# Matmuls of a hybrid mixer layer read their moving operand alternately from two halves

## The chip, the cores and the metric

The kernel is one program on one core of a Trainium2 chip. A core has TensorE (PE, with its weight loads listed as PEld), VectorE (DVE), ScalarE (ACT), GpSimd (POOL) and SyncE (SP), 16 DMA engines, the on-chip memory SBUF and the accumulation memory PSUM, which PE writes and DVE and ACT read. The metric is the device time of one execution in microseconds, as the median of several runs on the same chip.

## The reference

One layer over 512 positions of 1024 channels, in float32. Cut to what matters:

```python
h = rms_norm(x, norm_mix)
u_pool, u_lru, q, k, v, g_logits = split(h @ w_in)          # 8192 columns
gates = sigmoid(g_logits + b_gate)                           # three branches of 1024
y_pool = pool_mixer(u_pool, w_pool, pool_scale)              # causal means of 2, 4, 8, 16, minus the token
y_lru  = rglru_mixer(u_lru, conv_w, ...)                     # causal conv of width 4, two gates, linear scan
y_sb   = stick_breaking_attention(rms(q), rms(k), v)         # 8 heads of 128, strictly causal
merged = sum(gates[b] * (y[b] @ w_branch[b]) for b in range(3))
x = x + merged @ w_out
h2 = rms_norm(x, norm_ffn)
x = x + (silu(h2 @ w_ffn_gate) * (h2 @ w_ffn_up)) @ w_ffn_down   # 2816 hidden channels
```

## The kernel before

Everything is kept with channels on the 128 partitions and the 512 positions along the row, except q, k and v, which are made with positions on the partitions. Every operand is split into a high part (rounded to `float32r`) and the rest; a product is three matmuls, high x high, high x low and low x high (`mm3`, L277 to L280). ACT makes the high part of a weight tile (L111, L1403) and DVE the rest (L112, L1404). A full chunk (`chan_chunk`, L365) is 2 output tiles x 8 blocks of the inner dimension x 3 matmuls, 48 in all, each with a weight load of 128x128 and a moving operand of 128x512.

The stages follow each other on PE without a break. The times are those of the profile:

- From 5.7 us: the first two gate chunks at L701, then two more by chunks, on the unnormalised input; `gate_store` (L563) scales the result by the norm and takes the sigmoid.
- From 50.2: four chunks of the linear recurrence (`lru_chunk`, L596), with four gate chunks in between. The causal convolution reads the chunk's PSUM tile: L602 once, then L609 three times for each of two rows, shifted by 1, 2 and 3 positions. The small gates are half-height matmuls at L626, two side by side, read by ACT at L630 and L631.
- From 144.9: q, k and v in seven block products each in place of eight (`tok_product`, L788, matmuls at L798, read by `snap` L808 on ACT and `final` L813 on DVE).
- From 260.2: the third branch's gates in seven block products (`product`, L282, matmuls of 256 columns at L287).
- From 298.8: pooling chunks (`pool_chunk`, evacuated at L942, mapped by `pool_back`, L959) and two branches' projections (`branch`, merged by DVE at L379 and L383), with attention spread among them: transposes (L1018), scores (L1040, read by two sigmoids at L1050 and L1051), a reversed scan (L1054), transposes of the weights (L1067), the output (L1079, copied at L1082).
- From 488.2: the third branch's projection in seven block products, 256 columns at L1238.
- From 528.7: the output projection (read at L1291), and from 570.5 the first two chunks each of the hidden gate and hidden up projections (`fg`, `fu`, read at L1473 and L1475), during which the normalised hidden operand is made on DVE (L1336) and split.
- From 614.7: nine chunk pairs of the hidden projections in seven block products, 256 columns at L287. From 786.5 the first part of the down projection, 512 columns by `mm3`, read at L1580; from 797.6 the rest in seven block products, 256 columns at L1611.

The order is that of the program. Side work is put in queues (`bg`, `abg`) and taken from them a step at a time between groups of matmuls (`tick`, L329). Weight tiles are made ahead by `emit_next` (L261): load on SP's queue, split on ACT and DVE, three buffers deep. Readers that free a PSUM tile soon have a raised priority. Offsets within the tiles (L35 to L39) fix where operands lie.

Of the kernel before, what the change touches and what calls it, by code (L numbers as in the profile page):

```python
# [16 lines left out]
P = 128  # L17
# [50 lines left out]
def layer_kernel(ctx: ExitStack, tc: tile.TileContext, x, xt, vecs, w_in, w_qkv7, w_gate7, w_pool, w_rg, w_ig,  # L68
# [24 lines left out]
    def cols(ap, k0, nk, c0, nc_):  # L93
        return ap[k0 * P:(k0 + nk) * P, c0:c0 + nc_].rearrange("(k p) c -> p k c", p=P)

# [181 lines left out]
    def mm3(ps, lh, ll, rh, rl, start, stop, skip=False):  # L277
# [94 lines left out]
    def merge(br, c, pss, gts):  # L372
        for j in range(2):
            if br == BRANCHES[0]:
# [4 lines left out]
                dve.tensor_tensor(m, pss[j], gts[j], ALU.mult)  # L379
                merged.append(m)  # L380
            else:
                m = merged[2 * c + j]
                dve.tensor_tensor(gts[j], pss[j], gts[j], ALU.mult)  # L383
# [24 lines left out]
    with ExitStack() as first:  # L408
# [154 lines left out]
        def gate_store(br, c, pss, scaled):  # L563
            gt = b4([2, S], f"gt{br}{c}")
            for j in range(2):
                g = pss[j]
                if not scaled:
                    dve.tensor_tensor(gt[:, j, :], g, rb, ALU.mult)
                    g = gt[:, j, :]
                act(gt[:, j, :], g, AF.Sigmoid, bias=vcol("b_gate", 8 * br + 2 * c + j))  # L570
# [7 lines left out]
        def load_lru_weights():  # L578
# [3 lines left out]
            for n, src in enumerate((w_rg, w_ig)):  # L582
                bd = src.rearrange("(t two) i j -> two i t j", two=2)
                for two in range(2):
                    q, o = LH[two], LH[(n + two) % 2]
                    nc.sync.dma_start(raw[q, :, o], bd[two])
# [6 lines left out]
            for two in range(2):  # L593
                nc.sync.dma_start(bigx[LH[1 - two], :], big[LH[two], :])

        def lru_chunk(c):  # L596
# [3 lines left out]
            with tc.high_priority(EARLY):  # L600
                for j in range(2):
                    dve.tensor_scalar(xc[:, j, :], pair[:, j, :], vcol("conv_w", 24 + 2 * c + j),  # L602
# [17 lines left out]
            def gates(j):  # L620
                ct = 2 * c + j
                ps = pb.tile([P, 2, S], F32, tag="mm", name=f"lg{c}{j}")
                for n, (w, x_) in enumerate((("h", "h"), ("h", "l"), ("l", "h"))):
                    for two in range(2):
                        q = LH[two]
                        nc.tensor.matmul(ps[:, two, :], lw[w][q, ct, :], st[x_][q, j, :],  # L626
                                         start=n == 0, stop=n == 2)
                for two in range(2):
                    q, o = LH[two], LH[1 - two]
                    act(st["r"][q, j, :], ps[q, two, :], AF.Sigmoid, bias=vcol("b_rg", ct)[q, :])  # L630
                    act(st["i"][q, j, :], ps[o, two, :], AF.Sigmoid, bias=bigx[o, ct:ct + 1])  # L631
# [64 lines left out]
        for k in range(KT):  # L696
            if k % 2 == 0:
                wh, wl = weights("first", k // 2)
            for w, x_ in ((wh, 0), (wl, 0), (wh, 1)):
                for n in range(4):  # L700
                    nc.tensor.matmul(pss[n // 2][n % 2], w[:, k % 2, n * P:(n + 1) * P], hu[k][x_],  # L701
# [86 lines left out]
        def tok_product(t, nm, ps, first):  # L788
            bh, bl = BQ[WITH[nm]]
            for i in range(2):  # L790
                ah, al = weights("seven", t, nm, i)
                tick()
                for a in range(2):
                    ts_ = slice(a * P, (a + 1) * P)
                    for kk in range(2):
                        k = 2 * i + kk
                        for n, (b_, a_) in enumerate(((bh, ah), (bh, al), (bl, ah))):
                            nc.tensor.matmul(ps[:, a, :], b_[:, k, ts_], a_[:, kk, :],  # L798
# [4 lines left out]
        for t in VKQ:  # L803
# [4 lines left out]
            def snap(key, src):  # L808
                r[key] = b4([2, 512], f"r{t}{key[0]}{key[1]}")
                with tc.high_priority(EARLY):  # L810
                    act(r[key], src, AF.Copy, scale=-1.0 if key[0] else 1.0)

            def final(key, src):  # L813
                dve.tensor_tensor(r[key], r[key], src, ALU.subtract if key[0] else ALU.add)
# [89 lines left out]
    with ExitStack() as mix:  # L904
# [35 lines left out]
        def evac_u(ps, name):  # L940
            u = slot(name)
            act(u, ps, AF.Copy)  # L942
# [16 lines left out]
        def pool_back(g, j):  # L959
# [9 lines left out]
            act(yh, ps, AF.Copy, scale=sc)  # L969
            dve.scalar_tensor_tensor(yl, ps, sc, yh.bitcast(F32), ALU.mult, ALU.subtract)  # L970
# [32 lines left out]
        def head_tasks(h):  # L1003
# [28 lines left out]
            def scores(a):  # L1032
# [3 lines left out]
                for i in ZORDER[a]:  # L1036
# [3 lines left out]
                    mm3(z[:, c0:c0 + w], qh[:, ii], ql[:, ii], kh[:, 0:w], kl[:, 0:w], True, True)  # L1040
# [6 lines left out]
                for i in ZORDER[a]:  # L1047
                    _, c0, n = ZSEG[i]
                    cs = slice(c0, c0 + n)
                    act(K[:, cs], z[:, cs], AF.Sigmoid, scale=qrs[:, 1, i, h:h + 1])  # L1050
                    act(A[:, cs], z[:, cs], AF.Sigmoid, scale=qrs[:, 0, i, h:h + 1])  # L1051
# [21 lines left out]
            def yout():  # L1073
                ps = paux.tile([P, S], F32, tag="aux", name=f"py{h}")
                vh, vl = st["v"]
                for n, k in enumerate((0, 1, 2, 3)):
# [3 lines left out]
                        n == 0, n == 3)  # L1080
                ysb[h] = slot(f"ysb{h}")
                act(ysb[h], ps, AF.Copy)  # L1082
# [609 lines left out]
```

## Time and profile before

| what | value |
|---|---|
| runs | 897.85, 899.41, 897.85 us; median 897.85 |
| span of the profiled execution | 896.5 us (first to last instruction); 1.35 us below the median of the runs, which holds what lies around the span |
| PE, weight loads, DVE, ACT busy | 99%, 89%, 82%, 59% of the span |
| granted TensorE clock | full in every slice |
| matmuls | 5563, of which 2186 have 512 columns of `float32r` |
| DMA | 154.08 MB, mean 172 GB/s |

The profile gives one execution. A busy share counts the union of an engine's instructions; matmuls overlap their successors, so the distance from one start to the next tells more of PE than the duration (a matmul of 512 columns lasts 0.39 us by the page, though the next one starts long before). "Chain" is the work that ended last, followed back, and its pieces do not overlap. In a row of groups stand the line, engine, operation, the tiles written and read, shapes and count, then the busy time in us, the mean of one in ns, and the engine's idle time before them with what ended it.

### The profile page before, as it was taken

The page shows a single profiled execution, that of the slowest core. Times are in us where ns is not written, and L with a number is a line of the kernel's source. Part 1 is how long each engine was busy: PE and PEld are TensorE (multiplying, and loading weights), DVE is VectorE, ACT ScalarE, POOL GpSimd, SP SyncE. Part 2 cuts the span into 40 slices and gives each one's busy share as a digit, 9 for nine tenths or more (in the row PEclk, how much of TensorE's full clock was granted, in tenths as well). Part 3 has the DMA queues.
Part 4 walks back from the last instruction along what each step waited for, and adds up shares of the span by engine and source line. Part 5 has one row for each costly group of instructions (what it writes and reads, how often), then busy time and mean ns, then how long its engine had stood idle before and what let it go on. Part 6 is the DMA issues. An engine that isn't in the chain of part 4 may idle for free.

```text
span 896.5 us, 14227 instructions
## 1 busy us (share of the span) xinstructions
PE 891.2 (99%) x5563; PEld 795.2 (89%) x5563; DVE 739.4 (82%) x934; ACT 528.5 (59%) x730; POOL 88.8 (10%) x130
## 2 busy tenths in 40 slices
PE   9999999999999999999999999999999999999998
PEld 6888778788889888888888988889999999999998
DVE  6897897997786599967887695699988888899974
ACT  6554989546856556554664544545555555746642
POOL 1110002222323101000001100000000000021200
PEclk9999999999999999999999999999999999999999
DMA  9495336798692785734636865336443343897913
GB/s 337 141 297 167 118 114 215 217 302 252 174 276 72 217 252 175 236 108 152 205 90 154 179 190 170 106 107 169 126 131 104 95 118 97 228 243 195 186 42 118
DMA packets 116644, 154.08 MB, mean 172 GB/s; under 512 B 8161, under 2 KB 90081, under 8 KB 116577
## 3 DMA queue, kind: packets, MB, share of 16 engines
q1 hardware_dynamic: 103904, 107.30, 37.8%
q0 software_dynamic: 12528, 45.62, 21.6%
q8 instruction: 43, 0.70, 0.3%
q10 hardware_dynamic: 144, 0.26, 0.1%
q14 instruction: 25, 0.20, 0.1%
HBM read 132.71 MB, written 18.87 MB: 169 GB/s over the span
## 4 chain that ended last, share of the span: by engine, by line
PE 95%; DVE 2%; ACT 2%; issue 1%; DMA 0%; SPq 0%; DVEq 0%; ACTq 0%
PE ps_y L287 11%; PE ps_x L287 8%; PE ps_q L798 7%; PE ps_dy L1611 6%; PE ps_dx L1611 5%; PE ps_br L278 3%; PE ps_br L279 3%; PE ps_br L280 3%; PE ps_bY L1238 2%; PE ps_gate L701 2%; PE ps_gy L287 2%; PE ps_gate L280 2%; PE ps_bX L1238 2%; PE ps_gx L287 2%; PE ps_gate L278 2%; PE ps_gate L279 2%
## 5 line engine op out<-in xcount | busy, mean ns | idle before, releaser
L111 ACT ACTIVATE whi<-raw 128x1024 fp32r<-128x1024 f32 x69 | 73.1, 1060 | 85.2 <-PE ps_out L279 17.9
L112 DVE TENSOR_TENSOR wlo<-raw,whi 128x1024 fp32r<-128x1024 f32 x69 | 84.4, 1223 | 30.7 <-ACT whi L111 30.7
L112 DVE TENSOR_TENSOR wlo<-qw,whi 128x1024 fp32r<-128x1024 f32 x48 | 58.6, 1224 | 22.0 <-ACT whi L111 21.8
L111 ACT ACTIVATE whi<-qw 128x1024 fp32r<-128x1024 f32 x48 | 50.7, 1059 | 33.2 <-PE ps_q L798 15.3
L1403 ACT ACTIVATE wh_S<-w_S 128x1024 fp32r<-128x1024 f32 x36 | 38.3, 1067 | 34.4 <-PE ps_y L287 22.3
L1404 DVE TENSOR_TENSOR wl_S<-w_S,wh_S 128x1024 fp32r<-128x1024 f32 x36 | 43.8, 1222 | 5.2 <-ACT wh_S L1403 5.1
L1515 POOL DMA_DIRECT2D dw<-in_w_down_dram x20 | 16.9, 847 | 313.6 <-DMA dw<-in_w_down_dram 253.2
L1403 ACT ACTIVATE wh<-w 128x1024 fp32r<-128x1024 f32 x27 | 28.8, 1067 | 30.2 <-issue 11.9
L1404 DVE TENSOR_TENSOR wl<-w,wh 128x1024 fp32r<-128x1024 f32 x27 | 33.0, 1222 | 9.9 <-ACT wh L1403 9.9
L1403 ACT ACTIVATE whdS<-dw 128x1024 fp32r<-128x1024 f32 x20 | 21.3, 1067 | 22.5 <-PE ps_dy L1611 11.0
L1404 DVE TENSOR_TENSOR wldS<-dw,whdS 128x1024 fp32r<-128x1024 f32 x20 | 24.3, 1226 | 6.5 <-ACT whdS L1403 6.4
L1054 DVE TENSOR_TENSOR_SCAN E<-K,ahead 128x512 f32<-128x512 f32 (+3 forms) x32 | 25.4, 815 | 4.4 <-ACT K L1050 4.4
L278 PE MATMUL ps_br<-yHH,whi 128*128 128x512 f32 x64 | 25.3, 395 | 0.0
L278 PE MATMUL ps_lru<-HH,whi 128*128 128x512 f32 x64 | 25.2, 394 | 0.0
L278 PE MATMUL ps_br<-yph,whi 128*128 128x512 f32 x64 | 25.2, 394 | 0.0
L278 PE MATMUL ps_pool<-HH,whi 128*128 128x512 f32 x64 | 25.2, 393 | 0.0
L280 PE MATMUL ps_gate<-HH,wlo 128*128 128x512 f32 x64 | 25.0, 391 | 0.0
L278 PE MATMUL ps_gate<-HH,whi 128*128 128x512 f32 x64 | 25.0, 391 | 0.0
L279 PE MATMUL ps_br<-ypl,whi 128*128 128x512 f32 x64 | 25.0, 391 | 0.0
L280 PE MATMUL ps_br<-yph,wlo 128*128 128x512 f32 x64 | 25.0, 391 | 0.0
L279 PE MATMUL ps_br<-yHL,whi 128*128 128x512 f32 x64 | 25.0, 390 | 0.0
L279 PE MATMUL ps_pool<-HL,whi 128*128 128x512 f32 x64 | 25.0, 390 | 0.0
(737 smaller groups left out, 3448.5 us busy)
## 6 DMA issues: line engine op xcount, KB each, us to landing
raw<-in_w_in_dram SPq DMA_DIRECT2D x31, 512.0 KB, 5.3
qw<-in_w_qkv_dram SPq DMA_DIRECT2D x24, 512.0 KB, 7.4
dw<-in_w_down_dram POOLq DMA_DIRECT2D x20, 512.0 KB, 7.5
w<-in_w_ffn_gate_dram SPq DMA_DIRECT2D x36, 256.0 KB, 4.0
w<-in_w_ffn_up_dram SPq DMA_DIRECT2D x36, 256.0 KB, 4.6
raw<-in_w_branch_dram SPq DMA_DIRECT2D x16, 512.0 KB, 4.1
qw<-in_w_qkv_dram POOLq DMA_DIRECT2D x12, 512.0 KB, 7.7
qd<-r POOLq DMA_DIRECT2D x12, 512.0 KB, 7.9
```

The lines of the kernel that those rows point to most:

```text
L111: act(hi, raw, AF.Copy)
L112: dve.tensor_tensor(lo, raw, hi.bitcast(F32), ALU.subtract)
L278: nc.tensor.matmul(ps, lh, rh, start=start, stop=False, skip_group_check=skip)
L279: nc.tensor.matmul(ps, lh, rl, start=False, stop=False, skip_group_check=skip)
L280: nc.tensor.matmul(ps, ll, rh, start=False, stop=stop, skip_group_check=skip)
L287: nc.tensor.matmul(o, a_[a][:, w, k, :], b_[b][:, k, :], start=first and n == k == 0, stop=last and n == 2 and k == 3, skip_group_check=True)
L798: nc.tensor.matmul(ps[:, a, :], b_[:, k, ts_], a_[:, kk, :], start=first and n == k == 0, stop=n == 2 and k == 3, skip_group_check=True)
L1054: dve.tensor_tensor_scan(E[:, c0:c0 + n][:, ::-1], K[:, c0 + 1:c0 + n + 1][:, ::-1], ahead[:, S - n:][:, ::-1], 0.0, ALU.mult, ALU.add)
L1238: nc.tensor.matmul(o, ah[x_][:, w, k, :], b[k][y_], start=first_ and n == k == 0, stop=n == 2 and k == 3, skip_group_check=True)
L1403: act(h, src, AF.Copy)
L1404: dve.tensor_tensor(l, src, h.bitcast(F32), ALU.subtract)
L1611: nc.tensor.matmul(o, a_[a][:, w, k0 + k, :], b_[b][:, k, :], start=first and i == k == 0, stop=last and i == 2 and k == nk - 1, skip_grou ...
```

## The change

Every matmul of 512 or 384 columns, and those of 256 that share their PSUM tile with them in attention, reads its moving operand with its columns in another order. `il` turns a row of 512 columns into pairs: column 0 and 256, 1 and 257, and so on. In attention, where segments of 128 columns matter by themselves, the pairs are made within blocks of 128: 0 and 64, 1 and 65. The sums then lie in PSUM in that order. PE writes them contiguously, as before. Each DVE and ACT instruction that reads such a tile takes it in the old order again: `in_order` reads every second word for the first half and the words between for the second, and `two` gives the SBUF side the same shape, contiguous. The convolution's shifts cross from one half to the other, so each of its shifted sums becomes two instructions, one on both halves and one on the 1 to 3 columns at the seam. The matmuls of 256 columns at L287, L1238 and L1611, the transposes, the two sums of squares and the warm-up are left as they were. `two` was a loop variable and is renamed there.

```diff
+    def il(ap, b=H):
+        if b == H:
+            return ap.rearrange("p (a b) -> p b a", b=b)
+        return ap.rearrange("p (c a b) -> p c b a", a=2, b=b)
+
+    def in_order(ap, b=H):
+        w = ap.ndim == 3
+        if b == H:
+            return ap.rearrange("p w (b a) -> p w a b" if w else "p (b a) -> p a b", b=b)
+        return ap.rearrange("p (c b a) -> p c a b", a=2, b=b)
+
+    def two(ap, b=H):
+        w = ap.ndim == 3
+        if b == H:
+            return ap.rearrange("p w (a b) -> p w a b" if w else "p (a b) -> p a b", b=b)
+        return ap.rearrange("p (c a b) -> p c a b", a=2, b=b)
...
-    def mm3(ps, lh, ll, rh, rl, start, stop, skip=False):
+    def mm3(ps, lh, ll, rh, rl, start, stop, skip=False, b=H):
+        rh, rl = il(rh, b), il(rl, b)
...
-                            nc.tensor.matmul(pss[j], w[:, k % 4, j * P:(j + 1) * P], rhs[k][r],
+                            nc.tensor.matmul(pss[j], w[:, k % 4, j * P:(j + 1) * P], il(rhs[k][r]),
...
-                dve.tensor_tensor(m, pss[j], gts[j], ALU.mult)
+                dve.tensor_tensor(two(m), in_order(pss[j]), two(gts[j]), ALU.mult)
...
-                    for j in range(2):
-                        dve.scalar_tensor_tensor(xc[:, j, d:], u[:, j, 0:S - d],
-                                                 vcol("conv_w", 8 * (3 - d) + 2 * c + j),
-                                                 xc[:, j, d:], ALU.mult, ALU.add)
+                    for j in range(2):
+                        x_, u_ = two(xc[:, j, :]), in_order(u[:, j, :])
+                        for o, i in ((x_[:, :, d:], u_[:, :, 0:H - d]), (x_[:, 1, 0:d], u_[:, 0, H - d:])):
+                            dve.scalar_tensor_tensor(o, i, vcol("conv_w", 8 * (3 - d) + 2 * c + j), o,
+                                                     ALU.mult, ALU.add)
...
-                        nc.tensor.matmul(ps[:, two, :], lw[w][q, ct, :], st[x_][q, j, :],
+                        nc.tensor.matmul(ps[:, n2, :], lw[w][q, ct, :], il(st[x_][q, j, :]),
...
-                    act(st["r"][q, j, :], ps[q, two, :], AF.Sigmoid, bias=vcol("b_rg", ct)[q, :])
+                    act(two(st["r"][q, j, :]), in_order(ps[q, n2, :]), AF.Sigmoid, bias=vcol("b_rg", ct)[q, :])
...
-                            nc.tensor.matmul(ps[:, a, :], b_[:, k, ts_], a_[:, kk, :],
+                            nc.tensor.matmul(ps[:, a, :], b_[:, k, ts_], il(a_[:, kk, :]),
...
-                    act(r[key], src, AF.Copy, scale=-1.0 if key[0] else 1.0)
+                    act(two(r[key]), in_order(src), AF.Copy, scale=-1.0 if key[0] else 1.0)
...
-                dve.tensor_tensor(r[key], r[key], src, ALU.subtract if key[0] else ALU.add)
+                v = two(r[key])
+                dve.tensor_tensor(v, v, in_order(src), ALU.subtract if key[0] else ALU.add)
...
-            act(u, ps, AF.Copy)
+            act(two(u), in_order(ps), AF.Copy)
...
-                    mm3(z[:, c0:c0 + w], qh[:, ii], ql[:, ii], kh[:, 0:w], kl[:, 0:w], True, True)
+                    mm3(z[:, c0:c0 + w], qh[:, ii], ql[:, ii], kh[:, 0:w], kl[:, 0:w], True, True, b=64)
...
-                    act(K[:, cs], z[:, cs], AF.Sigmoid, scale=qrs[:, 1, i, h:h + 1])
+                    zs = in_order(z[:, cs], 64)
+                    act(two(K[:, cs], 64), zs, AF.Sigmoid, scale=qrs[:, 1, i, h:h + 1])
...
-                        n == 0, n == 3)
+                        n == 0, n == 3, b=64)
...
-                            dve.tensor_tensor(t, d, t, ALU.add)
+                            dve.tensor_tensor(two(t), in_order(d), two(t), ALU.add)
```

The readers left out here (`gate_store`, the second form of `merge`, `pool_back`, the residual sums at L1291, the products at L1473 and L1475, L1082) and the matmuls at L701 are changed in the same way.

More of the change, by code (lines that the diff above doesn't have):

```diff
@@ L583, in load_lru_weights @@
                 bd = src.rearrange("(t two) i j -> two i t j", two=2)
-                for two in range(2):
-                    q, o = LH[two], LH[(n + two) % 2]
-                    nc.sync.dma_start(raw[q, :, o], bd[two])
+                for n2 in range(2):
+                    q, o = LH[n2], LH[(n + n2) % 2]
+                    nc.sync.dma_start(raw[q, :, o], bd[n2])
             hi, lo = w4([8, P], "lwh", F32R), w4([8, P], "lwl", F32R)
@@ L592, in load_lru_weights @@
             big = vecs[:, VOFF["b_ig"]:VOFF["b_ig"] + 8]
-            for two in range(2):
-                nc.sync.dma_start(bigx[LH[1 - two], :], big[LH[two], :])
+            for n2 in range(2):
+                nc.sync.dma_start(bigx[LH[1 - n2], :], big[LH[n2], :])
         def lru_chunk(c):
```

39 lines of the change are left out of this document (20 added, 19 removed).

## The prediction

> **What bounds the kernel.** I read the page first: its busy line, its slices with the granted clock, and the chain that ended last.
>
> ```profile
> span 896.5 us, 14227 instructions
> PE 891.2 (99%) x5563; PEld 795.2 (89%) x5563; DVE 739.4 (82%) x934; ACT 528.5 (59%) x730; POOL 88.8 (10%) x130
> PEclk9999999999999999999999999999999999999999
> PE 95%; DVE 2%; ACT 2%; issue 1%; DMA 0%; SPq 0%; DVEq 0%; ACTq 0%
> ```
>
> PE is busy 99% of the span at full granted clock, and the chain is 95% PE. Busy alone proves little, since pipelined matmuls overlap, so I asked PE's list of waits next, and then the chain in order of time, whose pieces hold no overlap.
>
> ```profile
> PE warm_ps L422 <- DVE warm L301: 1.5, 1, 1.5
> PE ps_q L798 <- DVE wlo L112: 0.4, 1, 0.4
> PE ps_gate L701 <- ACT hu L437: 0.3, 1, 0.3
> ```
>
> ```profile
> 216.82 21.76 PE ps_q L798 x96
> 661.64 2.72 PE ps_x L287 x24
> 811.77 27.20 PE ps_dx L1611 x240
> ```
>
> Real waits are 2.2 us in all. A matmul of 512 columns follows another every 21.76/96 = 0.2267 us, one of 256 columns every 27.20/240 = 0.1133 us: 0.4427 ns a column in both. The kernel is bound by the rate at which PE takes columns. That rate looks impaired. The nine warm-up matmuls give a slower pace to compare with (the view of instructions in time, at two places):
>
> ```profile
> 1.86 1.06 PE L422 MATMUL warm_ps<-warm 128*128 128x512 bf16 x2
> 3.99 0.63 PE L422 MATMUL warm_ps<-warm 128*128 128x512 bf16 x1
> ```
>
> ```profile
> L422 PE MATMUL warm_ps<-warm 128*128 128x512 bf16 x9 | 4.0, 625 | 1.5 <-DVE warm L301 1.5
> L1067 PE MATMUL pw<-idn,A 128*128 128x128 f32 x80 | 10.0, 272 | 0.0
> ```
>
> By the group row they start (4.0 - 0.625)/8 = 0.42 us apart, so five steps lie between 1.86 and 3.99: 0.426 us each, 0.832 ns a column. The transposes of L1067 come in eight bursts of ten, 1.25 us each, so (1.25 - 0.272)/9 = 0.1087 us apart, 2.2 ns above 128 columns of that pace (0.1065). The fast matmuls are nearly, but not quite, twice as quick: half of 0.426 is 0.213, and 0.2267 is 6.4% more. That half is the true fast pace is an estimate of mine from these rows; none shows it reached. The loss goes with the columns: at 256 columns there are twice as many weight loads per column and the same 0.4427. It does not go with DMA traffic either: in the first row of this table of stretches the DMA engines moved 231 GB/s, in the fourth 132 GB/s, and a matmul takes 115.3/506 = 0.228 and 44.2/196 = 0.226 us.
>
> ```profile
> 144.90:260.20 115.30, 114.89 (x506) 94.45 (x505) 100.97 (x106) 79.62 (x104) 31.85 (x34) 1.00 0.79 231
> 298.80:488.20 189.40, 189.36 (x962) 160.75 (x961) 156.32 (x270) 107.29 (x203) 10.81 (x20) 1.00 0.60 177
> 528.70:570.50 41.80, 41.80 (x187) 34.60 (x186) 26.06 (x30) 16.43 (x21) 0.00 (x0) 1.00 0.51 164
> 570.50:614.70 44.20, 44.20 (x196) 36.34 (x195) 41.39 (x56) 23.32 (x27) 0.00 (x0) 1.00 0.48 132
> 786.50:797.60 11.10, 11.10 (x52) 9.21 (x51) 11.10 (x16) 5.38 (x9) 3.13 (x4) 1.00 1.04 271
> 50.20:144.90 94.70, 94.68 (x434) 75.92 (x433) 77.25 (x89) 71.61 (x88) 7.00 (x10) 1.00 0.58 188
> ```
>
> Columns here: stretch, its us, then busy us and instructions of PE, weight loads, DVE, ACT and POOL. So what falls behind is either the reading of the 4-byte moving operand or the writing of the sums, both one word a column. The transposes, also 4-byte, show only 2.2 ns of it at half the pace: a supply that is nearly, not quite, fast enough.
>
> **The change on PE.** It removes and adds no matmul; it alters the order in which the columns are read: column 0, 256, 1, 257 and so on (within 128-column blocks, 0, 64, 1, 65). By the loops, 30 chunks of 48 matmuls, 96 at L701, 504 at L798, 48 each in the pool maps and the first down product, and 24 each in scores and attention output make 2184 changed matmuls of 512 columns. The 48 half-height ones of L626 run in pairs and add 24 places: 2208. There are 48 of 384 columns, and 96 of 256 in attention. The other 3020 or so of 256 columns are left, so the stretches from 614.7 to 786.5 and from 797.6 on do not move.
>
> What one altered matmul takes no row of before shows, since every moving operand there is contiguous. The ends: 0.213 us, half the warm-up's step, if the loss goes away; 0.426 to 0.435 (four times 0.1087), if every jump to the other half costs a column time; and 0.2267 if the order does not matter. I take the fast side, and there 0.2155: the floor of 0.213 plus the 2.2 ns that the transposes show above their pace. The reason, an assumption: with two streams in turn, a reader has twice the time to have the next words of each at hand, and a supply short by 6% is what that would mend; the weight loads stay out of the way, since at 256 columns they already fit into 0.1133 us each. The sum: 11.2 ns x 2208 = 24.7 us; for 384 columns three quarters, 8.4 ns x 48 = 0.4 us; for 256 columns nothing, as the weight loads may bind at 0.1133. Together 25.1 us. At the floor, 13.7 ns x 2208 = 30.2 us.
>
> The Trainium skill, "TensorE: Matmul & The Clock Gate", section Back-to-back issue gap, gives N/2.4 + 2.5 ns for a warm isolated matmul, 215.8 ns at 512 columns. This trace's 226.7 does not agree, and if the new order reached the page's figure the estimate would be 10.9 ns x 2208 = 24 us, close to the sum above.
>
> **The change on the readers.** Every DVE and ACT instruction that reads such a PSUM tile now reads it at a step of two words and writes or reads its SBUF side in order. No row shows such a step. The nearest ones are these (merge, final, snapshot, attention output, and the same scan forward at L681 and backward at L1054):
>
> ```profile
> L379 DVE TENSOR_TENSOR m<-ps_br,g 128x512 f32<-128x512 f32 x8 | 5.5, 688 | 3.2 <-PE ps_br L280 3.2
> L814 DVE TENSOR_TENSOR r<-r,ps_q 128x1024 f32<-128x1024 f32 x9 | 11.0, 1218 | 1.2 <-PE ps_q L798 1.2
> L811 ACT ACTIVATE r<-ps_q 128x1024 f32<-128x1024 f32 x9 | 9.2, 1027 | 6.8 <-PE ps_q L798 6.2 <-DVE r L814 0.6
> L1082 ACT ACTIVATE ysb<-py 128x512 f32<-128x512 f32 x8 | 4.8, 594 | 5.7 <-PE py L280 5.7
> L681 DVE TENSOR_TENSOR_SCAN li<-lt,ls 128x512 f32<-128x512 f32 x8 | 9.5, 1216 | 0.1
> L1054 DVE TENSOR_TENSOR_SCAN E<-K,ahead 128x512 f32<-128x512 f32 x8 | 9.8, 1220 | 0.7 <-ACT K L1050 0.7
> ```
>
> DVE spends (1218 - 688)/512 = 1.04 ns on a further column, ACT (1027 - 594)/512 = 0.85. Ends: nothing (the backward scan costs no more than the forward one, so a pattern other than unit step is not dear as such), or twice the time a column. By twice, DVE gains 112 readings of 512 columns x 0.53 = 59 us (16 in merge, 8 at L568, 32 in the convolution, 24 at L814, 8 each at L970, L1291, L1473/L1475 and L1580) and ACT 128 x 0.43 = 55 us. I take nothing, after the scan rows, and keep the other end as a rival.
>
> The convolution (L609) becomes two instructions for each of 24, the second on 1 to 3 columns. The nearest row is this one:
>
> ```profile
> L954 DVE SCALAR_TENSOR_TENSOR pw<-pw,invpos 128x3 f32<-128x3 f32 x2 | 0.3, 164 | 0.1
> ```
>
> 24 x 0.16 = 3.9 us of DVE, in the stretch from 50.2 to 144.9, where DVE has 17 us free now and some 12 when PE is quicker by 5. It waits for nothing of its own and only stands ahead of other DVE work, weight splits among it; I cost it at nothing there.
>
> **What is late next.** A quicker PE asks for splits and evacuations sooner. From 144.9 to 260.2 DVE has 101 us of work and PE would need 504 x 11.2 ns = 5.6 us less, 109.7: it fits. From 298.8 to 488.2 there are 33 us of room. Two stretches have none. From 570.5 to 614.7 DVE has 41.4 us of 44.2, which PE would cross in 42.0, and the hidden operand's eight normalised blocks and their splits must be done before L287 begins; I charge 1.5 us of the 2.2 gained. From 786.5 to 797.6 DVE is full, so the 0.5 us gained there are lost. ACT (80 of 115 us at its next busiest) and the DMA engines (0.79 of the time from 144.9 to 260.2, which becomes 0.83) do not bind. Net: 25.1 - 1.5 - 0.5 = 23.1, and I round the gain down to 22.5 for waits of some tenths at starts of groups such as L798's 0.4.
>
> The profiled span is 896.5; the median of the three runs is 897.85, so 1.35 us lie outside the span. 896.5 - 22.5 + 1.35 = 875.4.
>
> **Rivals.**
> 1. *Half of it, or the readers eat it.* Either only half the loss goes (5.6 ns x 2208 = 12.4 us: 886 with the same charges), or the readers double while PE gains in full: from 50.2 to 144.9 DVE would have 77 + 17 + 4 = 98 us for 90 (8 lost), from 144.9 to 260.2 101 + 13 = 114 for 110 (4 lost), from 570.5 on 45.6 for 42 (3.6, of which 1.5 are charged), in 786.5 to 797.6 another 4: about 875.4 + 18 = 893. For the half: nothing says that the supply is lifted whole. 885 to 896.
> 2. *The order does not matter to PE,* because the loss is on the side of the sums, written contiguously before and after. The 2.2 ns of the transposes fit this as well. Then 897.85 and some tenths for new waits: within 0.2%.
> 3. *PE gains nothing and the readers double.* Then DVE has 98 us for 94.7 in the first of those stretches (3), 45.6 for 44.2 (1.4) and 15.3 for 11.1 (4): about 906. Between 900 and 912.
> 4. *The other side: the jump costs.* If the reader keeps one line of the moving operand at hand, each column throws it away, and a column takes the warm-up's or the transposes' 0.83 to 0.85 ns. Then 512 columns take 0.426, +0.1997 x 2208 = +441 us, 384 columns (0.320 against 0.170) +7, 256 columns (0.213 against 0.113) +10: about 1356. It decides as soon as a matmul takes more than 0.2267; each ns is 2.2 us. For it: the supply is already short with unit step. Against it: the transposes show that the shortage is small and only at the fast pace.
>
> The Trainium skill, "SBUF — State Buffer", section Door 1: The DMA port swizzle, says of the memory lines of 16 bytes that "each access that crosses to a new line pays a penalty", and here every access would cross; that is the fourth rival's mechanism, and no row of this trace can show it.
>
> **Chances.** The forecast (865 to 885) 0.52; first rival 0.14; second 0.06; third 0.10; fourth 0.18. Faster by over 0.2% (below 896; 0.2% is about what a measurement of this kernel can tell from no change) 0.66, within 0.06, slower 0.28. The range leaves the fourth out and goes from the floor without charges (897.85 - 30.6 = 867, with a little below) to the third: 866 to 910. The likeliest case's own range is 866 to 885.
>
> **What would show it.** In the changed profile the chain's piece of 96 ps_q matmuls would take 20.7 us (24 take 5.17); 20.5 is the floor, 21.76 the second or third rival, some 41 the fourth. The pieces of 24 ps_y and ps_x stay at 2.72. L814 stays near 1218 and L811 near 1027, or goes to some 2280 and 1900 if the step is dear. PE's waits should grow to a few us, on DVE, around L287's first tile and L280 at the first down product. I am wrong from the first step if ps_q's piece does not shrink.

## The result and the profile after

| kernel | median, us | runs | ratio to before, 95% interval |
|---|---|---|---|
| before | 898.32 | 897.85 to 899.41 | |
| after | 882.25 | 881.89 to 882.75 | 0.9819 (0.9805 to 0.9833) |

The change makes the kernel 16.1 us quicker (the median of before has one run more in it than the table ahead of the prediction). The forecast was 875.4, a gain of 22.5, with a range of 866 to 910: the sign and the mechanism on PE were right, and 6.4 us of the gain did not come.

First the page of after: the span, the busy line and the shares of the chain by engine.

```profile
span 881.0 us, 14269 instructions
PE 868.6 (99%) x5563; PEld 798.1 (91%) x5563; DVE 740.9 (84%) x958; ACT 525.7 (60%) x730; POOL 90.9 (10%) x130
PE 78%; DVE 11%; ACT 6%; DMA 2%; issue 2%; SPq 1%; ACTq 0%; DVEq 0%
```

PE is still called 99% busy, which says little. The chain says more: it was 95% PE and is 78% PE now, with 17% on DVE and ACT. The chain in order of time holds the altered matmuls (the first line) and, below them, a piece of 256 columns that was left alone:

```profile
176.31 20.72 PE ps_q L818 x96
613.99 2.72 PE ps_x L305 x24
```

An altered matmul now follows another every 20.72/96 = 0.2158 us in place of 0.2267; one of 256 columns still takes 2.72/24 = 0.1133. Next the readers, in groups by line and shape (busy us, then the mean of one in ns):

```profile
L397 DVE TENSOR_TENSOR m<-ps_br,g 128x512 f32<-128x512 f32 x8 | 5.5, 686 | 1.5 <-PE ps_br L298 1.4
L835 DVE TENSOR_TENSOR r<-r,ps_q 128x1024 f32<-128x1024 f32 x9 | 11.0, 1219 | 0.7 <-PE ps_q L818 0.6
L831 ACT ACTIVATE r<-ps_q 128x1024 f32<-128x1024 f32 x9 | 9.2, 1026 | 6.1 <-PE ps_q L818 5.3 <-DVE r L835 0.8
L1104 ACT ACTIVATE ysb<-py 128x512 f32<-128x512 f32 x8 | 4.7, 592 | 5.2 <-PE py L298 5.2
L630 DVE SCALAR_TENSOR_TENSOR xc<-ps_lru,vt,xc 128x510 f32<-128x510 f32 x8 | 6.0, 747 | 0.0
L630 DVE SCALAR_TENSOR_TENSOR xc<-ps_lru,vt,xc 128x3 f32<-128x3 f32 x8 | 1.8, 220 | 0.0
```

Against 688, 1218, 1027 and 594 ns of before, the step of two words costs nothing. New is the last row, the convolution's seam: 220 ns each. Last, the list of PE's waits (total, times, longest):

```profile
PE ps_q L818 <- DVE wlo L129: 2.3, 2, 1.2
PE ps_gate L298 <- DVE wlo L129: 2.2, 1, 2.2
PE warm_ps L440 <- DVE warm L319: 1.5, 1, 1.5
PE ps_br L296 <- ACT up L963: 1.4, 1, 1.4
PE ps_x L305 <- DVE wl_S L1426: 0.7, 1, 0.7
PE ps_q L818 <- ACT r L831: 0.4, 1, 0.4
PE z L297 <- DVE qkl L1043: 0.3, 1, 0.3
PE pq L1039 <- DMA at<-qd: 0.2, 1, 0.2
PE pq L1039 <- DVE wtl L1092: 0.2, 1, 0.2
```

Before there were three rows and 2.2 us. The account: (21.76 - 20.72)/96 = 10.8 ns on 2208 places is 23.9 us. By the starts in the trace, the 48 matmuls of 384 columns went from 175 to 163 ns (0.6 us) and the 96 of 256 in attention from about 120 to 112 (0.8). PE's own work is thus about 25.3 us shorter, and the span 15.5. **Some 10 us are new time in which PE waits or runs slowly.** The rows above sum to 9.2 us, 7.0 more than the three of before. A row counts from the modelled end of the matmul before the wait; from start to start a wait costs some 0.16 us more (2.38 for the 2.22 at the gate), which makes it a little over 8 us. A table of stretches shows most of the rest:

```profile
119.50:122.60 3.10, 3.10 (x9) 2.42 (x8) 3.10 (x4) 1.10 (x2) 0.76 (x1) 0.50 0.83 229
```

Behind the gate's wait of 2.2 us the granted clock (the 0.50) was half; by the trace's record of the clock from 119.4 to 122.8, for 3.4 us, in which the matmuls start up to 0.43 us apart. Some 1.7 us are lost by it. What makes PE wait at that gate is seen in the instructions in time:

```profile
103.19 1.28 ACT L675 ACT_TABLE_LOAD   x1
105.83 1.28 ACT L681 ACT_TABLE_LOAD   x1
108.22 1.23 DVE L686 SCALAR_TENSOR_TENSOR lt<-lr,lt 128x1024 f32<-128x1024 f32 x1 [3.86 <-ACT ls L681]
110.09 1.04 ACT L128 ACTIVATE whi<-raw 128x1024 fp32r<-128x1024 f32 x1
112.54 4.77 DVE L630 SCALAR_TENSOR_TENSOR xc<-ps_lru,vt,xc 128x510 f32<-128x510 f32 x12
117.22 1.22 DVE L129 TENSOR_TENSOR wlo<-raw,whi 128x1024 fp32r<-128x1024 f32 x1
118.50 0.48 PE L298 MATMUL ps_gate<-HH,wlo 128*128 128x512 f32 x1 [2.22 <-DVE wlo L129]
```

DVE stands idle for 3.86 us while ACT works through an exponential and a root with two loads of their tables, then does what had queued up, the convolution among it (4.77 us; 4.02 before), and only then the low part of the weights that PE needs, though ACT's high part of them was there at 111.1. Before, DVE stood idle at this place too, 4.4 us. Nearly all was in time there: the split was done at 121.6 and PE asked for it at 121.4. Now PE asks 5.3 us sooner, at 116.1, and the split is done only 3.1 us sooner, at 118.4.

### The profile page after: what moved, and what is told of

It is laid out like the page before. It is cut to its first block, busy times and chain, and to the rows that moved or that the text cites. A ratio compares the mean times of both kernels' runs of the same rounds, so it can differ in the third digit from the quotient of the medians.

```text
span 881.0 us, 14269 instructions
## 1 busy us (share of the span) xinstructions
PE 868.6 (99%) x5563; PEld 798.1 (91%) x5563; DVE 740.9 (84%) x958; ACT 525.7 (60%) x730; POOL 90.9 (10%) x130
## 4 chain that ended last, share of the span: by engine, by line
PE 78%; DVE 11%; ACT 6%; DMA 2%; issue 2%; SPq 1%; ACTq 0%; DVEq 0%
PE ps_y L305 10%; PE ps_x L305 8%; PE ps_q L818 7%; PE ps_dy L1633 6%; PE ps_dx L1633 5%; DVE wlo L129 3%; PE ps_br L296 3%; PE ps_br L297 3%; PE ps_br L298 3%; PE ps_bY L1260 3%; PE ps_gate L721 2%; PE ps_gy L305 2%; PE ps_bX L1260 2%; PE ps_gx L305 2%; ACT whi L128 1%
## 5 line engine op out<-in xcount | busy, mean ns | idle before, releaser
L128 ACT ACTIVATE whi<-raw 128x1024 fp32r<-128x1024 f32 x69 | 72.8, 1055 | 80.1 <-PE ps_out L297 16.1
L1425 ACT ACTIVATE whdS<-dw 128x1024 fp32r<-128x1024 f32 x20 | 21.3, 1065 | 22.5 <-PE ps_dy L1633 11.0
L296 PE MATMUL ps_gate<-HH,whi 128*128 128x512 f32 x64 | 25.1, 392 | 0.0
L297 PE MATMUL ps_gate<-HL,whi 128*128 128x512 f32 x64 | 24.9, 389 | 0.0
L297 PE MATMUL ps_lru<-HL,whi 128*128 128x512 f32 x64 | 24.3, 379 | 0.0
L298 PE MATMUL ps_lru<-HH,wlo 128*128 128x512 f32 x64 | 24.3, 379 | 0.0
```

The lines of the kernel that those rows point to most:

```text
L128: act(hi, raw, AF.Copy)
L296: nc.tensor.matmul(ps, lh, rh, start=start, stop=False, skip_group_check=skip)
L297: nc.tensor.matmul(ps, lh, rl, start=False, stop=False, skip_group_check=skip)
L298: nc.tensor.matmul(ps, ll, rh, start=False, stop=stop, skip_group_check=skip)
L1425: act(h, src, AF.Copy)
```

## The experiments

Theory after the result: PE's supply of columns has two streams, one for the odd and one for the even columns of an instruction, and the lost 10 us are PE arriving early at places where DVE or ACT was late by a fixed amount. Rivals: any order other than unit step would do; the readers or the seam cost the rest; the waits belong to the edits and not to the pace. In every table of orders "places" are addresses in the moving operand.

**e1: twenty-one orders of the moving operand.** Each of the 21 block products of q, k and v has its own order.

```diff
-    nc.tensor.matmul(ps[:, a, :], b_[:, k, ts_], il(a_[:, kk, :]),
+    PATS[t, nm](ps[:, a, :], b_[:, k, ts_], a_[:, kk, :],
+    # e.g. rearrange("p (c a b) -> p c b a", a=2, b=8), "p (b a) -> p a b", "p (a b c) -> p b a c"
```

> The changed kernel, but each of the 21 block products of q, k and v (24 matmuls of 512 columns each) reads its moving operand in an order of its own, and the readers are left as they are, so that positions come out shuffled. Orders: unit step; two places in turn at a distance of 256, 64, 32, 16, 8, 4 and 2 words; one place with a step of 2, 4, 8, 16 and 32 words; four and eight places in turn; two halves in turn in runs of 2, 4, 8, 16, 32 and 64 words. Theory (two streams): the loss of 11 ns is a shortage at the read of one running place, and two places far apart in turn make it up. Then two, four and eight places at 64 words and more give 0.216 us a matmul, unit step 0.2267; a step in one place gives 0.2267 or more; long runs go back towards 0.2267, and places 2 or 4 words apart stay at 0.2267, as both lie in the same stretch of memory. Rival (any other order): whatever is not unit step gives 0.216, a step of 2 to 32 words and places 2 words apart included. Rival (jump with a price at some distances): one of the orders takes 0.3 to 0.43 us.

The median distance of two starts, ns for 512 columns:

| order | ns |
|---|---|
| unit step | 227 |
| two places in turn, 256, 64, 32, 16, 8 or 4 words apart | 216 |
| two places in turn, 2 words apart | 227 |
| one place with a step of 2, 4, 8, 16, 32 words | 452, 461, 431, 434, 435 |
| four places in turn, eight places in turn | 283, 487 |
| two halves, in runs of 2, 4, 8, 16, 32, 64 columns | 328, 254, 245, 240, 236, 227 |

Pieces of the chain of this kernel, for 24 matmuls each: 4 words apart, 2 words apart, one place with a step of 2 and of 4 words (the whole kernel, with all these orders in it, took 922.5 us).

```profile
175.66 5.18 PE ps_q L815 x24
180.84 5.47 PE ps_q L816 x24
186.30 10.87 PE ps_q L817 x24
197.18 11.07 PE ps_q L818 x24
```

The first row holds the order with 4 words between the places (5.18/24 = 0.2158), the second that with 2 (0.228). "Any other order will do" fell. The two streams are right in kind and were wrong in two guesses: 4 words are far enough apart, and four or eight places are not as good as two. And the fourth rival of the prediction, that a jump has its price, is true of one place that jumps, which takes twice as long; it is not true of two places in turn.

**e2: the same question for 256 columns.** The hidden projections' nine chunk pairs get nine forms, for the moving and for the stationary operand.

```diff
-    nc.tensor.matmul(o, a_[a][:, w, k, :], b_[b][:, k, :],
+    FORMS[form](o, a_[a], w, k, b_[b][:, k, :],   # form = the pair's number; halves of 128 or blocks of 64,
+                                                  # stationary columns with a step of 2, 3, 4 or 8
```

> The changed kernel, but each of the nine chunk pairs of the hidden projections (168 matmuls of 256 columns) reads its operands in a form of its own; readers are left, so positions and channels come out shuffled, and the stationary reads with a step take words of other blocks of the same tile. Forms: both as they are; moving operand from two halves of 128 in turn; stationary with a step of 2 words; both of these; stationary step 4 with moving halves; moving places 64 words apart; stationary step 8 with moving halves; stationary step 4 alone; stationary step 3 with moving halves. Theory (the weight load binds as well): 0.1133 us stays with the moving operand alone, and falls to 0.108 to 0.110 only where a step of the stationary read relieves the load too. Rival (only the moving read binds): halves alone bring 0.108 to 0.110. Rival (neither): 0.1133 in all, or more with the steps of 4 and 8, if the stationary read pays for a jump; 0.2 would be a load that takes twice the time.

Pieces of its chain, 24 matmuls each: as it is, moving operand from two halves of 128, stationary operand with a step of 2, and of 4 with the halves:

```profile
616.04 2.72 PE ps_y L311 x24
618.76 2.68 PE ps_y L312 x24
637.51 2.89 PE ps_y L313 x24
677.56 5.66 PE ps_y L315 x24
```

Two halves take 111.7 ns against 113.3, and so do places 64 words apart. Stationary columns with a step of 2 take 120 (118 with the halves), of 4 235 with the halves or without, of 3 175 and of 8 240 (both with the halves only). (The whole kernel took 956.2 us.) The theory had put the halves alone at 113.3 and the rival at 108 to 110; the result lies between. So the 256-column matmuls have a part of the same loss, about 1.7 ns each, and below that the weight load may bind: where it is made dearer, it sets the pace.

**e9: are they two lanes?** A second table, all from one tile of 1024 words.

```diff
+    # two places D words apart: a[:, 0:2*D].rearrange("p (a d) -> p d a", a=2)[:, 0:256, :]
+    # two places with a step:   a[:, 0:512].rearrange("p (a b s) -> p s b a", a=2, s=2)
+    # a start off the line:     a[:, 1:513]
```

> A second table of orders for the 512-column matmul, again one for each of the 21 q/k/v block products, all from the start of a tile of 1024 words (so these products read other numbers, and their result is not that of the reference). Places in turn: two at distance 256 (known: 0.2158), then 257, 258, 259, 260, 264, 272, 320 and 512 words; unit step from word 1 and from word 2; two places at 256 from word 1 and from word 2; two places at 256 that each go on by 2, 4 and 8 words; four places at 129 and at 132, eight at 68 (at 128 and 64 they took 0.283 and 0.487); one place with step 2 (known: 0.452). Theory, two lanes: the even and the odd columns are fetched by separate readers, and each wants its own columns close together, whatever their distance from the other's. Then every distance and every start takes 0.2158, a start off the line changes nothing, and two places with steps of their own of 2 words go at 0.216 to 0.23, since a lane in unit step goes by 2 words too, with steps of 4 and 8 at about twice. Rival, banks: it is the distance that matters, the two places must lie in unlike banks or at a whole number of lines of 16 bytes; then 257, 258 and 259 differ from 256, 260 and 264, by 5% or by more, and four places at 132 or eight at 68 are quicker or slower than at 128 and 64 by over 10%.

| order | ns |
|---|---|
| two places 256, 257, 258, 259, 260, 264, 272, 320, 512 apart | 216, 216, 217, 216, 216, 216, 216, 216, 216 |
| unit step from word 0, 1, 2 | 227, 237, 235 |
| two places 256 apart, from word 1, 2 | 216, 215 |
| two places, each with a step of 2, 4, 8 | 227, 452, 461 |
| four places 129 and 132 apart, eight 68 apart | 234, 272, 440 |

Pieces of its chain, 24 matmuls each: two places from word 2, then two places with steps of 2, 4 and 8:

```profile
213.57 5.19 PE ps_q L822 x24
218.75 5.46 PE ps_q L823 x24
224.21 10.87 PE ps_q L824 x24
235.09 11.08 PE ps_q L825 x24
```

The whole kernel took 914.1 us. This is the sharpest result. Look at each lane, that is, at every second column. In unit step a lane goes on by 2 words; in "two places with a step of 2" it does too, and both take 227. One place with a step of 2 and two places with a step of 4 both move a lane by 4 words: 452 and 452. One with a step of 4 and two with a step of 8 move it by 8: 461 and 461. Only where a lane goes on by 1 word is it 216. e1's places 2 words apart fit too: there a lane goes on by 1 and by 3 words in turn, and it is 227. Otherwise the distance of two places does not matter, so the rival's banks are ruled out for two. The theory missed once: unit step from word 1 or 2 is 8 to 10 ns slower than from word 0, while two places do not mind the start. With four and eight places the distance does matter (283 at 128 words, 234 at 129, 272 at 132), and why is open.

**e5: the readers alone.** The matmuls keep the old order.

```diff
-        if b == H:
-            return ap.rearrange("p (a b) -> p b a", b=b)
-        return ap.rearrange("p (c a b) -> p c b a", a=2, b=b)
+        return ap
```

> The changed kernel with every matmul reading in unit step again, while all readers keep their step of two and the convolution its seam, so that positions come out shuffled. Theory (the whole gain is the order on PE, the readers' step is free): matmuls of 512 columns at 0.2267 us, and 898.3 to 899.5, the time before plus little for the seam, which has more cover again. Rival (the readers' step costs, and hides part of the gain): 901 to 906, with DVE or ACT ending PE's waits. If part of the gain came from the readers: below 897.

899.0 us, ratio 1.0007 (0.9998 to 1.0016): nothing. One row is new among PE's waits:

```profile
PE ps_gate L296 <- DVE wlo L127: 0.7, 1, 0.7
```

So the readers' step is free, and the seam costs 0.7 us at the gate even at the old pace. All of the gain is PE's order, and the other new waits of after, which are absent here, come with PE's pace.

**e3: without the seam.** The second instruction of each shifted sum is left out.

```diff
-    for o, i in ((x_[:, :, d:], u_[:, :, 0:H - d]), (x_[:, 1, 0:d], u_[:, 0, H - d:])):
+    for o, i in ((x_[:, :, d:], u_[:, :, 0:H - d]),):
```

> The changed kernel without the 24 small instructions at the seam of the convolution (the sums of the first 1 to 3 positions of the second half lack the terms from the first half). Theory (the seam costs): those 24 x 0.22 = 5.3 us on DVE make PE's wait of 2.2 us for a weight tile at the last but one gate chunk and the 3 us of half clock after it; without them PE does not stop there, and the time falls from 882.3 by 3 to 5 us, to 877 to 879. Rival (ACT's chain sets the pace there): DVE stood 3.9 us waiting for ACT's exponentials and roots just before, and the seam adds only 0.7 us to each of four convolutions; the time falls by 0.5 to 1.5 us, the wait shrinks by 0.7 us and half clock stays. The same to within 0.3 us if the seam is hidden.

880.52 us (880.02 to 881.17), 1.7 below after, between the theory's range and the rival's. Two rows of its waits:

```profile
PE ps_gate L298 <- DVE wlo L129: 1.6, 1, 1.6
PE pq L1039 <- POOL ahead L941: 1.4, 1, 1.4
```

The gate's wait is 0.6 us shorter (a convolution takes 0.75 less), and no stretch of half clock follows it in this profile. Together that is some 2.3 us, of which a new wait of 1.4 at the attention's transposes takes back a part. That the seam is most of the gate's wait fell: 1.6 of 2.2 us stay without it.

**e4: the recurrence's chunks in unit step.** Their 192 matmuls and the convolution go back to the form of before.

```diff
-    pair = chan_chunk(("lru", c), hn, 1, pb, True)
+    pair = chan_chunk(("lru", c), hn, 1, pb, True, b=None)      # il(ap, None) is ap
...
-    x_, u_ = two(xc[:, j, :]), in_order(u[:, j, :])
-    for o, i in (...): dve.scalar_tensor_tensor(o, i, ..., o, ALU.mult, ALU.add)
+    dve.scalar_tensor_tensor(xc[:, j, d:], u[:, j, 0:S - d], ..., xc[:, j, d:], ALU.mult, ALU.add)
```

> The changed kernel with the four chunks of the recurrence read in unit step again, and the convolution as it was before (six instructions instead of twelve). PE does 192 matmuls at 0.2267 instead of 0.2158, 2.1 us more; DVE does 3 us less. Theory (the seam costs): 882.3 + 2.1 - 3 to 5, that is 879 to 881. Rival (ACT's chain sets the pace there): PE's wait at the gate chunk shrinks by about as much as its matmuls grow, 881 to 882.5, and the half clock behind the wait goes if the wait falls under some 1.5 us. If the seam is hidden and nothing waits: 884.4.

881.51 us (881.18 to 887.42), ratio 0.9829 (0.9804 to 0.9854), 0.7 below after, which is not told apart from it; the rival's range.

```profile
PE ps_gate L300 <- DVE wlo L131: 0.8, 1, 0.8
```

The 192 matmuls lose 192 x 10.8 ns = 2.1 us again, and PE, arriving later and finding DVE earlier, waits 1.4 us less and keeps its clock. What is given and what is taken nearly cancel: in this stretch the pace of PE buys little, because DVE and ACT set the end.

**e7: the splits first.** The lead in priority of the weight splits over other work is raised.

```diff
-AHEAD = 200
+AHEAD = 320
```

> The changed kernel with one number altered: the priority of making weight tiles ahead is 320 in place of 200, which puts DVE's low parts of weights ahead of the convolution and of the recurrence's sums in DVE's order; no work is added or removed. Theory (the lost 8 us are PE waiting at a few places for weight parts that stand in DVE's queue behind other work): the waits at the gate chunk (2.4 us, with 1.9 of half clock behind it) and at the first two products of q, k and v (1.2 and 1.3) go, 876 to 878. Rival (DVE and ACT are simply full there): the waits move to other places, 881 to 883.

888.03 us (887.23 to 888.67), ratio 0.9886 (0.9873 to 0.9900): 5.8 us slower than after, and slower than the rival's 881 to 883 as well. The theory that the waits can be had by putting the splits first fell. Its longest waits:

```profile
PE ps_q L818 <- ACT r L831: 3.7, 2, 2.2
PE lg L646 <- DVE xch L635: 2.0, 1, 2.0
PE pq L1039 <- DMA at<-qd: 1.7, 1, 1.7
```

The gate's row is gone, and in its place PE waits for what the splits now stand ahead of: ACT's reading of the q/k/v tiles (in the trace two high parts of weights stand close ahead of it, at 150.4 and 151.9 us) and DVE's cast of the convolution (a split at 120.1). That the wait for a transfer has the same reason is likely, but not shown. Behind the wait of 2.2 us the granted clock is half again, for 3.4 us.

**e6: the 256-column matmuls too.** The 3024 at L305, L1260 and L1633 read from two halves of 128, and their readers take the step of two.

```diff
-    nc.tensor.matmul(o, a_[a][:, w, k, :], b_[b][:, k, :],
+    nc.tensor.matmul(o, a_[a][:, w, k, :], il2(b_[b][:, k, :]),     # "p (a b) -> p b a", a=2
...
-    dve.tensor_tensor(t, t, ps, ALU.add)
+    dve.tensor_tensor(par(t), par(t), nat(ps), ALU.add)
```

> The changed kernel, and the 3024 matmuls of 256 columns left out there read from two halves of 128 in turn as well, with all their readers adapted. The run with forms showed 0.1117 in place of 0.1133 us for that form. Theory (PE sets the pace in these stretches, with weight loads as the next bound): 3024 x 1.7 ns = 5.1 us less, 877 to 878. Rival (DVE, at 151 of 170 us from 601 to 771, falls behind): 879 to 882, with waits of PE for split weights. Slower than 882.3 if a reader of two tiles in turn at a step costs more than the 512 column ones did.

**874.94 us** (874.45 to 876.47), ratio 0.9748 (0.9734 to 0.9761): 7.3 below after, and the best of all kernels here. Chain and waits:

```profile
609.87 2.68 PE ps_x L318 x24
253.08 2.68 PE ps_gy L318 x24
```

```profile
PE ps_gate L311 <- DVE wlo L142: 2.2, 1, 2.2
```

3024 x 1.7 ns are 5.1 us, but the narrow matmuls give more. Over their four stretches (the third branch's gates, its projection, the hidden and the down projections) the profile of after needs 346.3 us and this one 339.8, 6.6 less. The 1.7 ns come from pieces that took 2.72 us for 24; the first pieces of a stretch took longer in after, as here at the gates, and take 2.68 now like the rest:

```profile
254.72 2.87 PE ps_gy L305 x24
```

The two profiles are 8.4 us apart. Nearly all that is left, 1.6 us, lies ahead of q, k and v: the gate's wait is as long as in after, but its matmuls go on 0.216 us apart behind it, without a stretch of half clock.

**e8: e6 and e7 together.**

> The two before together: narrow matmuls in turn from two halves, and weight parts first. If both act where they should, they add: 871 to 874. If the narrow gain hangs on slack of DVE that the other order takes away: 876 to 878.

882.58 us (880.59 to 884.38), ratio 0.9825 (0.9812 to 0.9839), 7.6 above e6: nearly the same waits as e7. Both expectations fell, with e7's.

**e10: e6, with three of the waits aimed at.** e4's edits, the evacuation L963 ahead of ACT's other work, and the recurrence's last decay moved from ahead of the third gates into the q/k/v products.

```diff
+    with tc.high_priority(EARLY):
         act(two(u), in_order(ps), AF.Copy)
...
-        for f, c in ((lru_decay, 2), (lru_decay, 3), (lru_input, 2)):
+        for f, c in ((lru_decay, 2), (lru_input, 2)):
...
-                    for f, c in ((lru_input, 3), (lru_scan, 2), ...
+                    for f, c in ((lru_decay, 3), (lru_input, 3), (lru_scan, 2), ...
```

> The 256-column matmuls read from two halves as well (the kernel with that edit alone had 874.9), and three edits aim at the named waits of PE: the first products of the LRU chunks keep the unit step and the convolution its six instructions (this took the wait at the gate from 2.4 to 1.0 us before), the branch's evacuation by ACT goes ahead of its other work (the wait of 1.6 us at 352), and the last decay of the LRU goes from the stretch ahead of the gates into the q/k/v products (so that ACT is free sooner; the waits of 1.2 and 1.3 us at 147 and 164). Theory, the waits are PE's loss and each can be had by taking its cause away: 874.9 less 1.4 at the gate and 1.6 at the branch, less some of the 2.5 at the first q/k/v products, plus 0.7 for 48 matmuls of the LRU pairs at the old rate: 871 to 873. Rival, the waits only move (as they did when the splits were put first): ACT and DVE are as full as before in those stretches, another wait takes the place, and it stays at 874 to 877.

875.93 us (875.63 to 877.06), ratio 0.9756 (0.9743 to 0.9770): no better than e6. The rival's range, not the theory's.

```profile
PE ps_q L832 <- DVE wlo L144: 2.0, 3, 1.1
PE ps_br L311 <- ACT up L978: 1.4, 1, 1.4
PE ps_gate L313 <- DVE wlo L144: 0.8, 1, 0.8
PE ps_gy L320 <- ACT gx L907: 0.5, 1, 0.5
```

The gate gives 1.4 us, and the 192 matmuls at the old pace cost 2.1 (the expectation counted only 48 of them, 0.7; that was a slip). The first products of q, k and v give 0.3, a new wait of 0.5 at the third branch's gates takes it, and the higher priority of L963 moved nothing: the branch's row is the same.

## Why the prediction was right or wrong

**The bound** was named rightly: the rate at which PE takes columns, and on the reading side. The second rival (the order does not matter) is out, and so is the first rival's first half, as 10.8 ns of the expected 11.2 came (its 886 should be some 887 by its own terms; nothing hangs on it). The fourth is out from both sides: e1 shows what a price of a jump would have been, 431 to 461 ns, close to the 426 of the rival, and shows that reading two places in turn does not pay it.

**The altered matmul** was put at 0.2155 us and takes 0.2158. That it was met to 0.3 ns is in part luck: the 2.2 ns above the floor were borrowed from the transposes, and no run shows that what remains is the same loss. The reason given, two streams with twice the time each, is borne out by e9's lanes as far as runs can: they show the pattern of prices, not the circuit. The Trainium skill, "TensorE: Matmul & The Clock Gate", section Back-to-back issue gap, with its 215.8 ns for 512 columns, agrees with the trace of after, as it did not with that of before. The Trainium skill, "SBUF — State Buffer", section Door 1: The DMA port swizzle, has a price on each access that crosses to a new line; e1's step of 2 words stays within a line at every second access and takes 452 ns, two places cross at every access and take 216, so here the measurement decides against the rule as it stands.

**The 256-column matmuls** were put at "nothing, as the weight loads may bind at 0.1133". That was wrong: the 96 altered ones in attention gained 0.8 us, e2 has 111.7 ns for the others, and e6 makes 6.6 us of it. (With 23.9, 0.6 and 0.8 us the three widths came to 25.3 where 25.1 were forecast; the misses cancel.) The equal 0.4427 ns a column at both widths, which the prediction itself quoted, spoke for the same cause at both; the reservation about the weight loads had no row.

**The readers** were put at nothing and cost nothing (e5), so the first rival's second half and the third rival are out.

**The seam** was put at 3.9 us of DVE that is hidden, on the ground of 12 us free in its stretch. It takes 3.0 us (0.75 in each of four convolutions), and it is not hidden: 0.7 us at the old pace (e5), 1.7 at the new with what follows it (e3).

**The step that failed is "What is late next".** It charged 2.6 us (1.5 at the start of the hidden projections, 0.5 at the down product and 0.6 of rounding); the new time is about 10. Its method was the sum over a stretch: from 144.9 to 260.2, 101 us of DVE in 109.7 "fits", yet PE waits 2.3 us (0.4 before) in the first 24 us of just this stretch, for splits that stand behind other work of DVE. The stretch from 50.2 to 144.9 with its 12 us free holds the gate's 2.2 and the half clock behind it; that from 298.8 to 488.2 with 33 us of room holds the branch's 1.4. Of the places that it did name, the hidden projections lost 0.7 us, some 10 us after their start, where 1.5 were charged, and the first down product lost nothing where 0.5 were: its 48 matmuls took 10.4 us in place of 10.9. So the term had the right sign, the wrong size and mostly the wrong places. The rows that would have told it were there: the idle times of DVE behind ACT's table loads in the trace of before, where an instruction that PE needs stands behind a long wait.

That e6 ends at 874.9, beside the 875.4 forecast for after, is chance: a term that was left out (6.6) and waits that were not seen.

**The half clock** was no term of the prediction. Six traces have a stretch of it behind a wait (after, e1, e2, e7, e8, e9), and they show when it comes. Each stretch lasts 3.41 us, and the stretch of full clock ahead of it is a whole number of these: 150.19 us in e7, 119.47 in e8, 112.64 in the other four (44, 35 and 33 times 3.41). So here the clock changes in steps of 3.41 us. In all six a wait of PE of 2.0 us (e8) or 2.2 (the others) lies whole inside the step that ends where the half clock begins. e7 has the wait of 2.0 us too, and e8 that of 2.2; there they lie across the border of two steps, and no half clock follows. e3's 1.6 us at the gate lie inside one step and are not enough. This fits every trace with a record of the clock (e6's has none); no run tests it alone. Where the steps begin differs between executions: two of e6's five have a mean clock of 0.998, what one such stretch makes, and take 875.9 and 876.5 us, the other three 874.5 to 874.9; in e7 it is 888.6 and 888.7 against 887.2 and 887.5. In after three of four have it, but the fourth, at 882.13, is not quicker, so how much of the medians' differences to after is owed to it stays open.

What else stays open is whether the branch's 1.4 us can be had at all; it was tried once, without effect.

## What to carry to other kernels

Where PE bounds a kernel with moving operands of `float32r`, try their order: two places in turn, each in unit step, cost nothing at the readers here and gave 4.8% of each 512-column matmul. Whoever quickens the engine that bounds has to go through the others' queues instruction by instruction at the places where that engine's operands are made: free time summed over a stretch did not show some 7 of the 10 us that were lost again. And where the other engines are nearly full, a priority may only choose who waits: with DVE busy 86 to 90% and ACT 70 to 76% in the stretches from 50 to 255 us, e7 and e8 were slower by it, and e10 was no quicker.

## What the runs showed of the hardware that was not expected

- A moving operand of `float32r` that jumps in one place, by 2 words or by 32, takes twice the time (431 to 461 ns for 512 columns), while jumping between two places at every column is quicker than reading straight on (216 against 227). Unit step is also slower from word 1 or 2 (237, 235) than from word 0.
- Stationary columns with a step of 2 words make a matmul of 256 columns take 120 ns, of 3 words 175, of 4 words 235, of 8 words 240, where unit step allows 113 (112 with the moving operand from two halves, as in the runs with 3 and 8).
- The granted clock fell to half for 3.41 us behind waits of PE of only 2.2 us (after and e7) and 2.0 us (e8), each whole inside one step of 3.41 us of the clock's record, and did not where such a wait lay across two steps. The Trainium skill, "TensorE: Matmul & The Clock Gate", section HAM oscillation — how this bites in real kernels, has idle gaps of over about 3.4 us as the ones to avoid; these traces show that shorter ones can do it.
